# The sigmoid of the output gates as exp(-ln(1 + exp(-z))), with one VectorE operation per tile

## The chip, the cores and the metric

The kernel runs on one core of one Trainium2 chip. A core has a matrix engine (TensorE, here PE, with its weight loads as PEld), a vector engine (VectorE, DVE), an engine for activation functions (ScalarE, ACT), a general engine (GpSimd, POOL), a sync engine that issues transfers (SP) and 16 DMA engines. Each engine works through a queue of its own in order and waits on semaphores for the others. The metric is the device time of one execution in microseconds; the median of the runs counts. The profile is that of one further execution.

## The reference

One decoder layer of width 1024 on one sequence of 2048 positions: a modulated RMSNorm, one input projection, two groups of heads (A: gated linear attention, B: sliding-window attention), one output projection, a gated residual and a last RMSNorm. Both groups' outputs pass a SiLU gate of their own, and that gate is what the change touches.

```
proj = einsum('bsd,de->bse', h, w_in)
gq, gk, gv, ga, gz, sq, sk, sv, sz = split_cols(proj, COL_SIZES)
z = einsum('bsr,rk->bsk', ga, w_decay) + b_decay
log_a = log_sigmoid(z) / GLA_GATE_TAU
o_gla = rmsnorm(gla_chunked(gq, gk, gv, log_a), g_gla_head)
o_gla = o_gla * silu(gz)
o_swa = sliding_window_sink_attention(rope(sq), rope(sk), sv, sinks)
o_swa = o_swa * silu(sz)
x = x + gate * einsum('bse,ed->bsd', concat([o_gla, o_swa]), w_out)
return rmsnorm(x, g_final)
```

gz and sz have 512 columns each, and silu(z) = z * sigmoid(z).

## The kernel before

The 2048 positions are worked in four units of 512. In each unit the input projection runs slot by slot (lines 30 to 42 and 55 to 56): qk0 and qk1, gv0 and gv1, gz0 and gz1 for group A, kv, sq0 and sq1, sz0 and sz1 for group B. Every product of fp32 matrices is made of three matmuls on parts: a high part h and a low part l of each operand (hh and hl for the activations, wh_ and wl_ for the weights). An h part is a rounded copy by ACT, the l part is a subtraction on DVE or POOL. In the first unit the weights are split as they arrive, and the parts are written to memory (wc); later units load the parts. During the last unit late_rows (line 561) loads the output gate's weights and w_out: wor is a piece of w_out as loaded, DVE multiplies it by the gate and subtracts for the low part (woy or wol). Then last_rows and out_tile do the output projection (py) and the last norm, 16 tiles of 128 positions.

The gate slots gz0, gz1, sz0 and sz1 come out transposed, two tiles of 128x512 per slot in PSUM (pt; po in the first unit), so there are 4 x 2 x 4 = 32 gate tiles in all. sink_gz and sink_sz give each to gate_evac (line 804), which copies it to z (the tile zs, six buffers), and makes sigmoid(z) in e (the tile ge, a single buffer). log_sigmoid (line 797) makes log(sigmoid(z)) = min(z, 0) - ln(1 + exp(-|z|)): one DVE instruction makes min(-z, z), ACT takes Exp and Ln, and a second DVE instruction makes the difference. A third ACT instruction, Exp, gives the sigmoid. The product with z is made on POOL for group B, and on DVE together with the head's weight for group A. The same log_sigmoid serves the decay (dz, de, line 935), where the logarithm itself is wanted.

Other names that the rows show: pq are transposed queries, qs their parts, psc the scores, s the scores in SBUF with the maximum mx, its negative nm and the sum den; ppt the transposed probabilities, ph and pl their parts, pp a masked copy of them, ppo their product with the values vs, o the output; kst the keys, pkr their transposes. In group A pk and kn are transposed keys, pc scores, sT their copy, pu the state's update, R and Q the state.

The order of the instructions is planned when the kernel is built. Every operation goes to an object (Order, line 88) with a price; for DVE 0.155 us and one 960th of a us per element of a partition, or one 1920th for a plain copy or an operation with one tensor operand, both in SBUF (lines 366 and 367). A list scheduler with these prices fixes each engine's queue, PE's as well, so that a new price or one instruction fewer can change the order anywhere behind it.

Of the kernel before, what the change touches and what calls it, by code (L numbers as in the profile page):

```python
# [11 lines left out]
AF = mybir.ActivationFunctionType  # L12
ALU = mybir.AluOpType
# [370 lines left out]
def layer_kernel(ctx, tc, x, xT, w_ada, w_gate, b_cols, b_gate, g_cols, c_cols, pos, inv_freq,  # L384
# [3 lines left out]
    V, A, G, SY = [Engine(od, e) for e in ("V", "A", "G", "SP")]  # L388
# [408 lines left out]
    def log_sigmoid(z, e):  # L797

        V.scalar_tensor_tensor(e, z, -1.0, z, op0=ALU.mult, op1=ALU.min)
        A.activation(e, e, AF.Exp)  # L800
        A.activation(e, e, AF.Ln, bias=1.0)
        V.scalar_tensor_tensor(e, z, 0.0, e, op0=ALU.min, op1=ALU.subtract)

    def gate_evac(ps, z, g=None):
        A.copy(z, ps)
        od.lift = 0
        e = near.tile([P, NB], F32, name="ge", tag="ge", bufs=1)
        log_sigmoid(z, e)
        A.activation(e, e, AF.Exp)
        if g is None:  # L810
            G.tensor_tensor(z, z, e, ALU.mult)
        else:
            V.scalar_tensor_tensor(z, z, g, e, op0=ALU.mult, op1=ALU.mult)
# [75 lines left out]
    def sink_gz(pair):  # L889
        def sink(ct, ps):  # L890
            z = near.tile([P, NB], F32, name="zs", tag="zs", bufs=ZS)
            h = 2 * pair + ct
            gate_evac(ps, z, gh[:, h:h + 1])
            gzs[pair, ct] = z
        return sink
# [152 lines left out]
    def sink_sz(kv):  # L1048
        def sink(ct, ps):
            z = near.tile([P, NB], F32, name="zs", tag="zs", bufs=ZS)  # L1050
            gate_evac(ps, z)
            szs[kv, ct] = z
        return sink
# [340 lines left out]
```

## Time and profile before

| | us |
|---|---|
| median of 3 runs | 862.0 (861.47 to 865.98) |
| the profiled execution, whole | 860.93 |
| its span, first to last instruction | 859.2 |
| PE busy in the span | 837.2 |
| DVE busy | 547.5 |
| ACT busy | 493.9 |
| POOL busy | 373.9 |

The span is what the rows speak of; the median lies 1.1 us above the time of the profiled execution. A busy time is the union of an engine's instructions. PE's matmuls overlap in the pipeline, so that the duration of a single one says more than its share of the time; what PE waits for is read from the idle time before a matmul and from the instruction that ended it.

### The profile page before, as it was taken

The numbers are of one execution on the slowest core, as the hardware profiler recorded it, in microseconds if no ns is written. First come the engines' busy times: TensorE is split into PE (matmuls) and PEld (weight loads), VectorE is DVE, ScalarE is ACT, GpSimd is POOL, SyncE is SP. The second block draws the span as 40 slices with busy tenths as digits, with TensorE's granted clock in tenths as the row PEclk, the third lists the DMA queues.
The fourth block names the chain that finished last, engine by engine and source line by source line (L and its number), as shares of the span: only waits on it lengthen the run. The fifth ranks groups of instructions, "written<-read, shape, count | busy, mean of one in ns | idle before, by whom it ended". The sixth has DMA issues, their size and how long they took to land. (4 is left out here: it accounts for less than half of the span.)

```text
span 859.2 us, 14608 instructions
## 1 busy us (share of the span) xinstructions
PE 837.2 (97%) x5150; PEld 733.6 (85%) x5150; DVE 547.5 (64%) x1014; ACT 493.9 (57%) x1214; POOL 373.9 (44%) x450
## 2 busy tenths in 40 slices
PE   8999999999999999999999999999999999999996
PEld 7798879889899888899898989888888788888886
DVE  6995689785555467655438786668767664444442
ACT  4668588894673679645538756455467443333332
POOL 4624256657254265734425664153325442222221
PEclk9999999999999999999999999999999999999998
DMA  8889898774443566554346646569493764444411
GB/s 335 342 309 328 347 340 287 249 250 142 166 164 119 184 209 246 196 174 158 127 172 204 258 163 209 206 216 347 167 317 125 263 208 148 147 147 144 143 70 50
DMA packets 75999, 179.91 MB, mean 209 GB/s; under 512 B 8419, under 2 KB 24854, under 8 KB 72726
## 3 DMA queue, kind: packets, MB, share of 16 engines
q1 hardware_dynamic: 74918, 178.93, 59.2%
q8 instruction: 41, 0.67, 0.3%
q14 instruction: 32, 0.26, 0.1%
q10 hardware_dynamic: 1008, 0.05, 0.1%
HBM read 134.78 MB, written 44.17 MB: 208 GB/s over the span
## 5 line engine op out<-in xcount | busy, mean ns | idle before, releaser
L425 PE MATMUL py<-woh,m 128*128 128x512 f32 (+2 forms) x528 | 161.5, 385 | 0.4 <-ACT zs L378 0.4
L425 PEld LDWEIGHTS py<-woh,m 128*128 128x128 f32 x528 | 98.5, 188 | 20.5 <-ACT zs L378 0.8
L425 PE MATMUL py<-wol,m 128*128 128x512 f32 (+2 forms) x264 | 101.9, 386 | 0.0
L378 POOL TENSOR_TENSOR r<-r,gf 128x512 f32<-128x512 f32 x31 | 45.4, 1466 | 118.3 <-ACT xr L378 118.3
L378 ACT ACTIVATE ge<-ge 128x512 f32<-128x512 f32 x96 | 60.5, 630 | 29.9 <-DVE ge L378 29.2
L425 PE MATMUL pn<-wh_sq,hh 128*128 128x256 f32 x256 | 73.1, 287 | 1.4 <-DVE vs L378 1.4
L425 PE MATMUL pn<-wh_gv,hl 128*128 128x272 f32 (+1 forms) x256 | 73.6, 288 | 0.0
L425 PE MATMUL pn<-wh_gv,hh 128*128 128x272 f32 (+1 forms) x256 | 73.6, 287 | 0.0
L425 PE MATMUL pn<-wl_gv,hh 128*128 128x272 f32 (+1 forms) x256 | 73.4, 287 | 0.0
L425 PE MATMUL pn<-wl_sq,hh 128*128 128x256 f32 x256 | 72.9, 286 | 0.4 <-DVE wl_sq L378 0.3
L425 PE MATMUL pn<-wh_sq,hl 128*128 128x256 f32 x256 | 72.6, 284 | 0.0
L378 DVE TENSOR_TENSOR r<-py,xr 128x512 f32<-128x512 f32 (+2 forms) x33 | 22.3, 675 | 65.1 <-PE py L425 65.1
L378 ACT ACTIVATE s<-s,nm 128x129 f32<-128x129 f32 x128 | 51.2, 401 | 17.7 <-DVE nm L378 17.0
L378 POOL TENSOR_TENSOR o<-o,zs 128x128 f32<-128x128 f32 x64 | 34.5, 560 | 54.5 <-DVE o L378 54.5
L425 PEld LDWEIGHTS py<-wol,m 128*128 128x128 f32 x264 | 49.6, 188 | 9.8 <-issue 0.2
L378 POOL TENSOR_TENSOR qr<-qr,rope 128x256 f32<-128x256 f32 x32 | 26.1, 832 | 64.9 <-DVE rope L378 64.9
L378 POOL TENSOR_TENSOR s<-s,den 128x512 f32<-128x512 f32 x32 | 36.3, 1136 | 38.9 <-DVE den L378 38.8
L425 PEld LDWEIGHTS pn<-wh_sq,hh 128*128 128x128 f32 x256 | 48.7, 191 | 2.8 <-issue 1.8
L425 PEld LDWEIGHTS pn<-wl_sq,hh 128*128 128x128 f32 x256 | 48.8, 191 | 1.9 <-DVE wl_sq L378 0.8
L378 POOL TENSOR_TENSOR xt<-xt,rstd 128x512 f32<-128x512 f32 x27 | 36.2, 1346 | 31.6 <-DMA xt<-in_xT 22.8
L425 PEld LDWEIGHTS pn<-wh_sq,hl 128*128 128x128 f32 x256 | 48.9, 191 | 0.4
L425 PEld LDWEIGHTS pn<-wh_gv,hh 128*128 128x128 f32 x256 | 48.6, 190 | 0.7
(258 smaller groups left out, 2522.7 us busy)
## 6 DMA issues: line engine op xcount, KB each, us to landing
xr<-in_x SPq DMA_DIRECT2D x32, 256.0 KB, 2.8
mr<-mixd SPq DMA_DIRECT2D x16, 512.0 KB, 4.0
out<-r SPq DMA_DIRECT2D x32, 256.0 KB, 2.3
wa<-in_w_ada SPq DMA_DIRECT2D x7, 1024.0 KB, 8.4
xn<-in_x SPq DMA_DIRECT2D x24, 256.0 KB, 4.2
xt<-in_xT SPq DMA_DIRECT2D x24, 256.0 KB, 4.2
wl_sz<-wc SPq DMA_DIRECT2D x12, 512.0 KB, 5.4
wh_sz<-wc SPq DMA_DIRECT2D x12, 512.0 KB, 4.7
```

The costliest lines, as they stand in the source:

```text
L378: return order.add(eng, lambda: real(*args, **kw), dur, ins, outs, lock=lock, nbytes=nbytes)
L425: return od.add("PE", lambda: T.matmul(o, l, r, start=start, stop=stop), dur, [l, r] + ([] if start else [o]), [bank if start and bank is ...
```

## The change

In gate_evac the call of log_sigmoid and the Exp behind it are replaced. One DVE instruction with one tensor operand makes max(z, -87) in e; ACT makes exp(-e), then ln(1 + that), then exp of the negative of that. The kernel's decay keeps log_sigmoid.

```
@@ -805,8 +805,11 @@
         A.copy(z, ps)
         od.lift = 0
         e = near.tile([P, NB], F32, name="ge", tag="ge", bufs=1)
-        log_sigmoid(z, e)
-        A.activation(e, e, AF.Exp)
+
+        V.tensor_scalar(e, z, -87.0, None, op0=ALU.max)
+        A.activation(e, e, AF.Exp, scale=-1.0)
+        A.activation(e, e, AF.Ln, bias=1.0)
+        A.activation(e, e, AF.Exp, scale=-1.0)
         if g is None:
             G.tensor_tensor(z, z, e, ALU.mult)
         else:
```

The planned order changes on every engine. Three places follow; a number behind a name is a buffer's.

The first is in the first unit, where the first low part of probabilities, pl, is made. DVE's queue ahead of it, before:

```order
L378 TENSOR_TENSOR wl_gz_486<-wr_gz_488,wh_gz_485 128x512
L378 TENSOR_TENSOR hl_4_392<-xt_4_393,hh_4_391 128x512
L378 TENSOR_TENSOR wl_gz_486<-wr_gz_489,wh_gz_485 128x512
L378 TENSOR_SCALAR nm<-mx 128x4
L378 SCALAR_TENSOR_TENSOR ge<-zs,ge 128x512
L378 TENSOR_TENSOR pl<-ppt,ph 128x512
```

And now:

```order
L378 TENSOR_TENSOR wl_gz_486<-wr_gz_489,wh_gz_485 128x512
L378 TENSOR_SCALAR nm<-mx 128x4
L378 TENSOR_TENSOR qs<-pq,qs 64x2x128
L378 TENSOR_TENSOR wl_gz_486<-wr_gz_490,wh_gz_485 128x512
L378 TENSOR_TENSOR hl_6_398<-xt_6_399,hh_6_397 128x512
L378 TENSOR_TENSOR pl<-ppt,ph 128x512
```

The gate's instruction is gone from there; a part of the queries and two parts that stood behind pl now stand ahead of it. PE's queue ahead of the matmul that reads this pl (pn is the projection, slot gv1), before:

```order
L425 MATMUL ppo<-ph,vs 128x512
L425 MATMUL pn_491<-wh_gv_415,hl_6_178 128x256
L425 MATMUL pn_491<-wh_gv_415,hh_7_181 128x256
L425 MATMUL pn_491<-wl_gv_416,hh_7_181 128x256
L425 MATMUL pn_491<-wh_gv_415,hl_7_182 128x256
L425 MATMUL pn_493<-wh_gv_415,hh_0_153 128x256
L425 MATMUL pn_493<-wl_gv_416,hh_0_153 128x256
L425 MATMUL ppo<-pl,vs 128x512
```

And now:

```order
L425 MATMUL pn_493<-wl_gv_416,hh_6_177 128x256
L425 MATMUL ppo<-ph,vs 128x512
L425 MATMUL pn_493<-wh_gv_415,hl_6_178 128x256
L425 MATMUL pn_493<-wh_gv_415,hh_7_181 128x256
L425 MATMUL pn_493<-wl_gv_416,hh_7_181 128x256
L425 MATMUL pn_493<-wh_gv_415,hl_7_182 128x256
L425 MATMUL ppo<-pl,vs 128x512
```

It was row 772 of PE's queue, at the beginning of the tile pn_493; it is row 817 now, behind that tile.

The second place is some 30 us earlier, on DVE, where the keys' low parts (kst_201 and kst_203) are made; what is removed and added there, in one piece:

```order
 L378 TENSOR_TENSOR v<-po_257,ort 128x512
+L378 TENSOR_TENSOR kst_201<-pkr,kst_200 64x512
 L378 TENSOR_TENSOR wl_sz_294<-wr_sz_298,wh_sz_293 128x512
 L378 TENSOR_TENSOR wl_sq_404<-wr_sq_405,wh_sq_403 128x512
 L378 TENSOR_TENSOR wl_sq_404<-wr_sq_406,wh_sq_403 128x512
-L378 TENSOR_TENSOR kst_201<-pkr,kst_200 64x512
 L378 TENSOR_TENSOR kst_203<-pkr,kst_202 64x512
-L378 SCALAR_TENSOR_TENSOR ge<-zs 128x512
+L378 TENSOR_SCALAR ge<-zs 128x512
+L378 TENSOR_TENSOR qs<-pq,qs 64x2x128
```

One of the two key parts moves ahead of three subtractions for weights, and a part of the queries follows the gate's instruction directly.

The third place is in the last unit, on DVE, where pieces of w_out (wor) are multiplied between the steps of the sliding-window attention, before:

```order
L378 TENSOR_TENSOR qs<-pq,qs 64x2x128 x2
L378 TENSOR_TENSOR wor_1252<-wor_1252,gate_1221 128x512
L378 TENSOR_TENSOR woy_1254<-wor_1252,wox_1253 128x512
L378 COPY_PREDICATED s<-up_ex,psc 128x2x128
L378 TENSOR_TENSOR qs<-pq,qs 64x2x128 x2
L378 COPY_PREDICATED s<-up_ex,psc 128x2x128
L378 TENSOR_REDUCE mx<-s 128x4
```

And now:

```order
L378 TENSOR_TENSOR qs<-pq,qs 64x2x128 x2
L378 COPY_PREDICATED s<-up_ex,psc 128x2x128
L378 TENSOR_TENSOR qs<-pq,qs 64x2x128 x2
L378 COPY_PREDICATED s<-up_ex,psc 128x2x128
L378 TENSOR_TENSOR wor_1252<-wor_1252,gate_1221 128x512
L378 TENSOR_REDUCE mx<-s 128x4
L378 TENSOR_SCALAR nm<-mx 128x4
L378 TENSOR_TENSOR woy_1254<-wor_1252,wox_1253 128x512
```

The product of the loaded piece goes from between the first and the second pair of qs to behind both.

## Rows read from the trace of the kernel before

**Rows 1.** The page's busy times: us, share of the span, instructions.

```profile
PE 837.2 (97%) x5150; PEld 733.6 (85%) x5150; DVE 547.5 (64%) x1014; ACT 493.9 (57%) x1214; POOL 373.9 (44%) x450
```

**Rows 2.** Busy time by stage: stretch, its length, engines' busy us, PE clock, DMA.

```profile
0.00:51.00 51.00, 47.02 (x237) 39.48 (x238) 42.26 (x71) 29.52 (x62) 25.10 (x35) 1.00 0.83 322
51.00:158.00 107.00, 101.23 (x729) 92.87 (x728) 82.37 (x145) 79.40 (x174) 46.52 (x51) 1.00 0.92 329
158.00:545.00 387.00, 386.61 (x2583) 345.47 (x2582) 243.86 (x471) 248.08 (x638) 198.18 (x260) 1.00 0.53 185
545.00:692.00 147.00, 141.63 (x882) 121.69 (x881) 104.19 (x191) 83.36 (x218) 58.02 (x74) 1.00 0.68 233
692.00:852.00 160.00, 160.00 (x723) 133.59 (x721) 73.10 (x135) 51.96 (x120) 46.10 (x32) 1.00 0.40 136
```

**Rows 3.** Waits of PE: matmul, who ended them, us in total, times, longest.

```profile
PE psc L425 <- DVE qs L378: 2.5, 4, 1.5
...
PE ppo L425 <- POOL pp L378: 1.6, 1, 1.6
PE ppo L425 <- DVE pl L378: 1.6, 1, 1.6
...
PE pn L425 <- DVE vs L378: 1.4, 1, 1.4
PE pq L430 <- DVE kst L378: 1.1, 1, 1.1
PE pk L430 <- DVE qk L378: 0.9, 1, 0.9
```

**Rows 4.** The gate tile's instructions: count, ns min/median/max, first and last start.

```profile
L378 ACT ACTIVATE ge<-ge x96: 613/632/647, 52.9 to 676.5; 128x512 f32<-128x512 f32 x96
L378 DVE SCALAR_TENSOR_TENSOR ge<-zs x32: 673/693/1784, 51.3 to 671.7; 128x512 f32<-128x512 f32 x32
L378 DVE SCALAR_TENSOR_TENSOR ge<-zs,ge x32: 673/691/1702, 55.2 to 673.8; 128x512 f32<-128x512 f32 x32
L378 DVE SCALAR_TENSOR_TENSOR zs<-zs,gh,ge x16: 728/752/1372, 57.8 to 677.2; 128x512 f32<-128x512 f32 x16
```

**Rows 5.** DVE with one operand: one in the timeline, then a group by line.

```profile
49.40 0.43 DVE L378 TENSOR_SCALAR rn<-rr 128x512 f32<-128x512 f32 x1
...
L378 DVE TENSOR_SCALAR r<-r,frr 128x512 f32<-128x512 f32 x15 | 8.2, 548 | 1.6
```

**Rows 6.** Busy time of the gate tile's instructions alone (DVE, ACT, POOL), by stage.

```profile
158.00:545.00 387.00, 44.63 (x50) 37.78 (x60) 13.62 (x10) 1.00 0.53 185
```

**Rows 7.** Timeline near 146: start, us, engine, instruction, [idle before and its end].

```profile
145.62 0.68 DVE L378 SCALAR_TENSOR_TENSOR ge<-zs,ge 128x512 f32<-128x512 f32 x1
146.22 0.68 DVE L378 TENSOR_TENSOR pl<-ppt,ph 128x512 fp32r<-128x512 f32 x1
...
146.95 0.50 PE L425 MATMUL ppo<-pl,vs 128*128 128x512 f32 x1 [1.57 <-DVE pl L378]
```

**Rows 8.** Timeline near 115, the keys' parts.

```profile
112.23 3.49 DVE L378 TENSOR_TENSOR wl_sq<-wr_sq,wh_sq 128x512 fp32r<-128x512 f32 x2
...
115.64 1.40 DVE L378 TENSOR_TENSOR kst<-pkr,kst 64x512 fp32r<-64x512 f32 x2
...
117.19 0.41 PE L430 MATMUL pq<-ident,qr 128*128 128x128 f32 x2 [1.09 <-DVE kst L378]
```

**Rows 9.** Timeline near 636, pieces of w_out between attention steps.

```profile
634.18 0.69 DVE L378 TENSOR_TENSOR wor<-wor,gate 128x512 f32<-128x512 f32 x1 [2.55 <-DMA wor<-in_w_out]
...
636.76 0.87 DVE L378 TENSOR_TENSOR qs<-pq,qs 64x256 fp32r<-64x256 f32 x2
...
637.23 0.51 PE L425 MATMUL psc<-kst,qs 128*128 128x256 f32 x2 [1.51 <-DVE qs L378]
```

**Rows 10.** Timeline near 92, the values' parts.

```profile
91.12 0.35 ACT L378 CAST vs<-pn 128x256 fp32r<-128x256 f32 x1
...
92.05 0.19 PEld L425 LDWEIGHTS pn<-wh_sq,hh 128*128 128x128 f32 x1 [1.60 <-issue]
92.08 0.36 PE L425 MATMUL pn<-wh_sq,hh 128*128 128x256 f32 x1 [1.44 <-DVE vs L378]
```

## The prediction

> **What bounds the kernel now.** First the page's busy times: TensorE (PE) is busy 837.2 of 859.2 us, 97% [rows 1]. Whoever looks for a gain has therefore 22 us of PE idle time to look at, and nothing else, as long as the matmuls stay what they are; the change leaves all of them. Next the busy time by stage [rows 2], where the reader is to subtract PE's busy time from each stretch. From 0 to 51 us, before the first gate tile, 4.0 us are idle (51.00 - 47.02). From 51 to 158, the rest of the first unit, 5.8. From 158 to 545, 0.4 in 387 us. From 545 to 692, the last unit with the loading of w_out beside it, 5.4. From 692 to 852, the output projection, nothing. The last 8 us are the closing normalisation. The change can reach the second, third and fourth stretch only: 11.6 us at most, a floor of about 850 for the median.
>
> Then the list of PE's waits [rows 3], which says who ends them. VectorE (DVE) ends most of what stands there: psc on qs 2.5, ppo on pl 1.6, pn on vs 1.4, pq on kst 1.1, pk on qk 0.9; one, ppo on pp 1.6, is ended by GpSimd. So DVE does matter, but at some ten places, not through its 64% share.
>
> **The edit itself.** Per gate tile, 32 of them, two DVE instructions with two operands go, of 693 and 691 ns at the median [rows 4]. One with one operand comes. The trace has that form at the same size, 128x512 in SBUF: 0.43 us in one row, and 548 ns on the mean of 15 that use a column as scalar [rows 5]. The new one's scalar is a constant, as in the first of the two, so I take 0.43. By medians DVE gets back 0.693 + 0.691 - 0.43 = 0.95 us per tile, 32 x 0.95 = 30.5 us in all. From above: at the longest seen, 1784 ns [rows 4], each new one would cost more than the two together, and DVE would get nothing; I don't take it, since the median is near the shortest (673).
>
> ScalarE (ACT) keeps three activations per tile at 632 ns [rows 4]: a scale of -1 for none, Exp and Ln as before, and the order of the instructions has the same three table loads. What falls away there is the trip to DVE and back between the second and the third. GpSimd (POOL) keeps its 16 products. A -87 clamp is a constant. All this I cost at nothing; it is covered by PE's work, and shown by the third stretch: 50 of the 80 DVE instructions on these tiles lie there, 44.63 us of them [rows 6], while PE idles 0.4 us. So most of what the edit saves is saved where nobody waits: at most 0.4 us of it counts.
>
> **What it moves.** The order of all instructions is planned with prices, and two cheaper instructions shift every engine's queue; the totals of work stay. So the sum goes by PE's waits, place by place.
>
> At 146.95 PE waits 1.57 us for pl [rows 7]. DVE runs ge there from 145.62 and pl right behind it, at 146.22: the removed instruction stood 0.60 us ahead of pl. Now wl_gz, hl and a qs stand ahead of it, but the matmul that reads pl has gone from row 772 of PE's queue to row 817. A PE row takes 386.61 / 2583 = 0.15 us on the mean of the third stretch [rows 2], so it comes some 6 us later: more than pl's delay by qs (half of 0.87, [rows 9]), a wl_gz and an hl (an estimate from the 3.49 us of two such subtractions, [rows 8]: 1.75 each) together, 3.9. I count -1.5.
>
> At 117.19 PE waits 1.09 us for kst, which stands behind two subtractions of 3.49 us [rows 8]. The first kst now goes ahead of those; the second doesn't, and the buffer that PE waits for is free after both. But the waiting transposes stand three matmuls later. Between nothing and all of it, 1.09, and with a wait for qs some 5 us behind it (0.5 of the 2.5 in [rows 3]) whose qs now stands right behind the gate tile's instruction: I count -1.2.
>
> At 637.23 PE waits 1.51 us for qs [rows 9]. Ahead of qs, DVE had been held until 634.18 by a load of w_out (2.55 us idle). Now that qs stands ahead of the load's product; the row maximum mx stays behind it. This wait goes, and mx takes its place as the late one; the transposes that need it come earlier in PE's queue than before. I count half, -0.75; between -1.5 and +2.5, the row's own hold.
>
> At 92.08 PE waits 1.44 us for vs [rows 10], a DVE subtraction that is late because ACT's cast is (91.12). In the new order vs stands even later, behind three more subtractions, but the matmul that waited for it has moved some 40 rows back. Instead the eight pairs of pu, which need kn, come at once; ACT makes kn where it made vs, at about 91.1, so PE waits until about 91.7 (one ACT copy of 0.6). I count -0.3.
>
> pk on qk, 0.9, and ppo on pp, 1.6 [rows 3], I leave: ahead of qk the product zs (752 ns) now stands in place of ge (691) [rows 4], and the order around pp hasn't changed on DVE or PE.
>
> Removed: 1.5 + 1.2 + 0.75 + 0.3 = 3.75 us. Against it stand the waits that a new order makes. The nearest rows are the list itself: waits of 1.1 to 1.6 us at the places where PE's queue runs close behind DVE. I take one of 1.3 us. Net -2.5 us. The sum is made against the profiled execution, span 859.2 and 860.9 in all; the median of the runs is 862.0, 1.1 above it. **859.5 us** for the median.
>
> **A rule that would give more.** Weight loads are busy 733.6 us, 85% [rows 1]. In the stretch from 692 to 852, where PE never waits, their share is 133.59 / 160 = 83% [rows 2]; so 85% is what a PE without waits shows, and no headroom. The Trainium skill, Perfetto Trace Analysis, section Identifying the Most-Contended Engine, calls the share of busy matmuls a bad measure and wants that of weight loads in its place; by that rule 126 us would be open, and a cheaper DVE could give far more than the floor above. The trace doesn't bear it out here, and I give it 0.01.
>
> **Rivals.** (1) *Nothing that lasts*, 0.22: each wait removed is made again nearby, since DVE is late there because loads and ACT are (the 2.55 us hold in [rows 9], the late cast in [rows 10]). For it speaks that only 0.60 us of the 5.4 and 5.8 us idle is seen to stand on the removed instruction itself [rows 7]. 862, between 861 and 863.5.
>
> (2) *DVE was late by its load alone*, 0.15: in the first unit DVE gets back up to eight tiles' 0.95 us, 7.6 in all, and its waits there and in the last unit go: 2.5 + 1.6 + 1.4 + 1.1 + 0.9 and pp's 1.6 behind pl [rows 3], 9.1 us. 853, or 856 when a third is kept. Against it speak the same two rows.
>
> (3) *Slower: PE's queue drawn too near to a DVE that a load holds*, 0.10. In the last unit the planner puts the transposes of s earlier in PE's queue, trusting DVE to have made them. But DVE's queue is in order, and a product that waits for its load of w_out holds all behind it, 2.55 us at one place [rows 9], with mx and what follows behind it now. At two loads of this kind, with the second unit's gains eaten: -2.5 is lost, and 2 x 2.55 = 5.1 comes on top: 867. It decides from the point where PE has less than a hold's length of other matmuls in front of those transposes.
>
> (4) *The change doesn't do what it says*, 0.03: the new instruction takes about as long as the two, at the 1784 ns of [rows 4]. Then DVE is loaded as before while the plan thinks it free: 862 to 864. The Trainium skill, SBUF - State Buffer, section on the two separate sides, says that a DVE instruction in a two-port mode and a GpSimd instruction keep each other out of a shared pair of ports for the whole instruction, as does one with two SBUF inputs. By that rule the new instruction can still be held by the whole of a GpSimd product; the long ends of [rows 4] fit it, the medians say that it is the exception.
>
> **How the numbers follow.** The forecast has the rest, 0.49, with a range of its own from 857.5 to 861.5. What this kernel's measurement can tell from no change is about 0.5%, 4.3 us. Faster by more: rival 2 (0.15), the weight-load rule (0.01) and a little of the forecast, 0.18. Slower by more, above 866.3: most of rival 3, 0.09. The same: 0.73. For 8 in 10 the range reaches from 855, which leaves a good half of rival 2 outside, to 866, which leaves most of rival 3.
>
> **What would show it.** DVE's instructions on the gate tile: 32 of about 0.43 us in place of 64, its busy time down by some 30 us; ACT, POOL and PE's busy time within a few us. PE idle in 158 to 545 still below 1 us. No wait for pl near 146 and none for qs near 637. A wait for kn near 92 in place of that for vs. In the last unit the reader should look for waits on s or qs behind a product of w_out: if they are above 2 us, rival 3 holds. I am wrong on the main point if PE's idle time from 51 to 692 changes by more than 5 us either way, or if the time moves while it doesn't.

## The result and the profile after

The changed kernel takes **854.5 us** at the median of 6 runs (853.26 to 855.31), beside 861.7 us for the kernel before in the same set (859.34 to 865.98): a ratio of 0.9913, 95% interval 0.9894 to 0.9932. It is faster by 7.3 us; the forecast was 859.5 and its range ended at 855.0. The profiled execution took 855.22 us, its span 853.5 us. Four executions among the experiments below, 6 to 92% longer than the others of their kernels at a lower granted clock (0.75 to 0.97, where the others have 0.99 to 1.00), are left out of the medians and ratios.

The page's busy times, which answer to [rows 1]:

```profile
PE 833.1 (98%) x5150; PEld 732.1 (86%) x5150; DVE 510.2 (60%) x982; ACT 493.6 (58%) x1214; POOL 367.4 (43%) x450
```

DVE has 37.3 us less, in 32 instructions fewer; ACT is where it was. The busy time by stage, for [rows 2] (stretch, its length, engines' busy us, PE clock, DMA):

```profile
0.00:51.00 51.00, 44.78 (x230) 37.14 (x231) 42.13 (x68) 28.22 (x60) 24.59 (x35) 1.00 0.81 309
51.00:158.00 107.00, 102.87 (x738) 94.56 (x738) 77.74 (x140) 81.18 (x173) 48.11 (x53) 1.00 0.94 340
158.00:545.00 387.00, 386.74 (x2596) 346.87 (x2594) 222.38 (x459) 247.35 (x642) 193.66 (x260) 1.00 0.54 187
545.00:692.00 147.00, 143.72 (x892) 124.15 (x891) 97.92 (x185) 86.21 (x223) 59.46 (x75) 1.00 0.71 241
```

Subtract PE's busy time again: 6.2, 4.1, 0.3 and 3.3 us are idle, where it was 4.0, 5.8, 0.4 and 5.4. Two things are to be seen. The first stretch, which the change doesn't touch, is slower in this execution than in that of before; the profile of before is the quickest there of all that were taken (the others are 0.2 to 2.1 us later at its end), so that is chance, and the profiles are compared from 51 us on. And behind 51 us the idle time falls by 1.6 + 0.1 + 2.1 = 3.9 us, while the time falls by 7.2: the start of the 237th matmul is 1.5 us later than before, the end is 5.7 us earlier. PE does the same 5150 matmuls in both. So 3.3 us came out of what the trace shows as busy. By stage, from the starts of the matmuls with equal numbers (the 965th, the 3545th, the 4425th): 2.0 us gained up to 158, 2.0 from there to 545, 3.2 up to 692, nothing behind. (A second profiled execution of the changed kernel gives 1.9, 1.6 and 3.9, so a stretch of one trace is known to some 0.7 us.)

PE's waits, for [rows 3] (from 51 to 692 us):

```profile
PE pz L425 <- POOL zs L378: 1.9, 1, 1.9
PE pk L430 <- DVE qk L378: 1.6, 2, 1.3
PE ppo L425 <- POOL pp L378: 1.5, 1, 1.5
PE psc L425 <- ACT s L378: 1.5, 1, 1.5
PE psc L425 <- DVE qs L378: 0.4, 1, 0.4
PE psc L425 <- DVE s L378: 0.3, 1, 0.3
PE pt L425 <- DVE wl_qk L378: 0.2, 1, 0.2
```

Gone are pl (1.6), vs (1.4), kst (1.1) and 2.1 of the 2.5 on qs. pp stands as it did, and pk has grown from 0.9 to 1.6. pz at 77.7 and psc at 138.5 are new. The gate tile's instructions, for [rows 4]:

```profile
L378 ACT ACTIVATE ge<-ge x96: 613/632/667, 53.1 to 667.4; 128x512 f32<-128x512 f32 x96
L378 DVE TENSOR_SCALAR ge<-zs x32: 410/428/1566, 52.7 to 664.7; 128x512 f32<-128x512 f32 x32
```

The median of the new instruction, 428 ns, is the 0.43 us that the prediction took.

### The profile page after: what moved, and what is told of

The parts are those of the page before. It is cut to its first block, busy times and chain, and to the rows that moved or that the text cites. A ratio compares the mean times of both kernels' runs of the same rounds, so it can differ in the third digit from the quotient of the medians.

```text
span 853.5 us, 14606 instructions
## 1 busy us (share of the span) xinstructions
PE 833.1 (98%) x5150; PEld 732.1 (86%) x5150; DVE 510.2 (60%) x982; ACT 493.6 (58%) x1214; POOL 367.4 (43%) x450
## 5 line engine op out<-in xcount | busy, mean ns | idle before, releaser
L378 ACT ACTIVATE ge<-ge 128x512 f32<-128x512 f32 x96 | 60.6, 632 | 16.5 <-DVE ge L378 15.5
L378 POOL TENSOR_TENSOR s<-s,den 128x512 f32<-128x512 f32 x32 | 34.2, 1072 | 48.7 <-DVE den L378 40.7
```

The costliest lines, as they stand in the source:

```text
L378: return order.add(eng, lambda: real(*args, **kw), dur, ins, outs, lock=lock, nbytes=nbytes)
```

## The experiments

Each is compared with the kernel before, run in the same set (862.5, 863.1, 861.9 and 861.9 us in the four sets). Five questions were asked.

**Are they the instructions or the order?** The change does both. To part them, the planner was told the old prices and the old operations, so that the queues of all engines are those of before, and only the instructions differ:

```
-        log_sigmoid(z, e)
-        A.activation(e, e, AF.Exp)
+        two = 0.155 + NB / 960     # the old price
+        V.tensor_scalar(e, z, -87.0, None, op0=ALU.max).dur = two
+        A.activation(e, e, AF.Exp, scale=-1.0)
+        A.activation(e, e, AF.Ln, bias=1.0)
+        od.add("V", lambda: None, two, [z, e], [e], lock=True)   # planned, not issued
+        A.activation(e, e, AF.Exp, scale=-1.0)
```

> The new instructions in the old order: every engine's queue is word for word that of the kernel before, only that the first DVE instruction of each gate tile has one operand and the second is not issued. Theory A (DVE's relief itself): the 30 us that DVE gets back count by themselves, most of the 7.3 us is here, 855 to 857. Theory B (the order): what was gained comes from the new queues; here only the waits directly behind a removed instruction shrink, near 146 from 1.57 to about 1 us and near 598 from 0.94 to about 0.3, so 860 to 861.

Measured: 857.3 us, ratio 0.9942 (0.9922 to 0.9962). The new instructions give 5.2 of the 7.3 us without a single row being moved. Its trace, 3.7 us shorter than that of before, gains 1.9 us up to 158, 0.8 from there to 545 and 1.2 up to 692, by the starts of the matmuls. The counterpart has the changed kernel's queues with the old instructions in them (the second one issued where the third activation stands):

```
-        V.tensor_scalar(e, z, -87.0, None, op0=ALU.max)
-        A.activation(e, e, AF.Exp, scale=-1.0)
+        V.scalar_tensor_tensor(e, z, -1.0, z, op0=ALU.mult, op1=ALU.min).dur = one
+        A.activation(e, e, AF.Exp)
         A.activation(e, e, AF.Ln, bias=1.0)
-        A.activation(e, e, AF.Exp, scale=-1.0)
+        third = A.activation(e, e, AF.Exp)   # issues the second DVE instruction ahead of itself
         ...                                  # not shown: how it does so; one is the new price
```

> The old instructions in the new order: queues as in the changed kernel, but each gate tile has its two DVE instructions of two operands again, the second one put where its third activation stands. Theory A: nothing of the gain is left, 861 to 864, slower where the plan draws PE close to a DVE that now has more to do. Theory B: most of the gain stays, 855 to 857.

Measured: 876.5 us, ratio 1.016 (1.013 to 1.019), far above the times of either theory (A allowed for slower, without a figure). PE's longest waits in its stretch from 158 to 545 us, where before has 0.4 us in all:

```profile
PE psc L427 <- DVE qs L380: 4.2, 6, 1.1
PE ppo L427 <- DVE o L380: 1.3, 1, 1.3
PE po L427 <- DVE o L380: 1.1, 1, 1.1
```

Waits for DVE appear in the stretch that I had taken for covered; by the starts of its matmuls the kernel loses 9.0 us there. The new order is no good by itself: it leans on the instructions being short. (It is one way to put the old instructions in; another place for the second could cost less.)

**Is it DVE's load, or the trip to DVE and back?** Three kernels in the order of before. The first leaves out the second instruction and keeps two operands in the first; the second makes the first cheap and keeps the second; the third keeps two instructions of the old form and size, but the second depends on nothing that ACT makes, nor does ACT wait for it.

```
e5  V.scalar_tensor_tensor(e, z, -87.0, z, op0=ALU.max, op1=ALU.max)
    ... od.add("V", lambda: None, ...)                     # second planned, not issued
e6  V.tensor_scalar(e, z, -87.0, None, op0=ALU.max).dur = two
    ... V.scalar_tensor_tensor(e, z, 0.0, e, op0=ALU.mult, op1=ALU.subtract)
e7  V.scalar_tensor_tensor(e, z, -87.0, z, op0=ALU.max, op1=ALU.max)
    ... nc.vector.scalar_tensor_tensor(z, z, 1.0, z, op0=ALU.mult, op1=ALU.min)
```

> All queues are word for word those of the kernel before, but the second of the two DVE instructions on each gate tile isn't issued; the first keeps its two operands (it makes max(z, -87) in the two-operand form). Theory A (DVE's load): the gain goes with the DVE time that is given back, 32 x 0.69 = 22 of the 30.5 us that gave 5.2 us with both edits in this order, so 0.72 x 5.2 = 3.8 us: 858.7 beside 862.5 for before. Theory B (the trip): what cost was that the second instruction stands on DVE's queue waiting for ACT's logarithm and holds all behind it (the trace of before has 15.0 us of DVE idle time in 12 waits of that kind): all of the 5.2 us comes, 857.3.

> All queues are those of the kernel before; the first DVE instruction on each gate tile has one operand (max(z, -87)) in place of two, the second stays with its two operands and its wait for ACT (it makes 0 * z - ln). Theory A: 32 x 0.26 = 8.4 us of DVE time come back, 0.28 x 5.2 = 1.4 us: 861. Theory B: nothing, 862 to 862.8, since DVE then waits longer for ACT.

> All queues are those of the kernel before and DVE does as many instructions of the same form and size on each gate tile (two with two operands, 128x512), but the second reads and writes z alone and depends on nothing that ACT makes, and ACT's third activation needs nothing of it. DVE's busy time stays at about 547 us. Theory A (load): no gain, 862 to 863. Theory B (the trip): most of the 5.2 us, 857.3 to 858.5.

Measured: 857.4 (ratio 0.9934, 0.9909 to 0.9959); 859.3 (0.9963, 0.9944 to 0.9981); 863.0 (1.0, 0.9982 to 1.0019). The third decides. First the wait of DVE's second instruction for ACT's logarithm in the trace of before (us, times, longest); then the third kernel's busy times, and the one wait for ACT's activations that DVE's instructions on the gate tiles still have there, that of the product zs:

```profile
DVE ge L378 <- ACT ge L378: 15.0, 12, 3.3
...
PE 838.7 (97%) x5150; PEld 735.1 (85%) x5150; DVE 549.0 (64%) x1014; ACT 492.8 (57%) x1214; POOL 374.4 (43%) x450
DVE zs L380 <- ACT ge L380: 3.9, 5, 2.6
```

The 15.0 us of waiting are gone, DVE's load is as before, and so is the time. Theory B falls: without the trip, and with the load kept, nothing was gained, within 1.6 us to either side. Theory A holds in kind. The busy times with the first instruction cheap, with the second left out, and with both (the first experiment):

```profile
PE 835.8 (97%) x5150; PEld 732.3 (85%) x5150; DVE 539.2 (63%) x1014; ACT 494.5 (58%) x1214; POOL 370.8 (43%) x450
...
PE 834.6 (98%) x5150; PEld 733.2 (86%) x5150; DVE 520.6 (61%) x982; ACT 493.5 (58%) x1214; POOL 369.2 (43%) x450
...
PE 836.3 (98%) x5150; PEld 733.6 (86%) x5150; DVE 512.5 (60%) x982; ACT 493.0 (58%) x1214; POOL 365.9 (43%) x450
```

A's proportion doesn't show: 8.3, 26.9 and 35.0 us less of DVE's busy time gave 3.8, 5.6 and 5.2 us by the medians, with intervals of 1.6 to 2.2 us to either side, and the first of them is more than twice what A expected. One rival isn't tested. GpSimd's busy time falls with DVE's, from 373.9 to 370.8, 369.2 and 365.9, though it does the same 450 instructions, and it stays at 374.4 in the kernel that gained nothing. A part of the relief may have reached PE through GpSimd, and no run parts the two.

**Does the covered stretch count?** New instructions in the order of before, on the 20 gate tiles between 158 and 545 us alone, and on the 12 others alone:

```
+        if 6 <= tile < 26:        # the other kernel: if not 6 <= tile < 26
             ...                   # the instructions of the first experiment
+        else:
+            log_sigmoid(z, e)
+            A.activation(e, e, AF.Exp)
```

> The queues of the kernel before, with the new instructions on the 20 gate tiles that lie between 158 and 545 us alone (one operand in the first, the second not issued); the other 12 keep theirs. By the prediction's step (at most 0.4 us of what is saved there counts, since PE idles 0.4 us there): 862.5 to 863, and PE's matmuls of that stretch take as long as before within 0.4 us. By its rival (short delays of PE hide in what the trace shows as busy, since matmul records overlap): the stretch gets 1 to 2 us shorter, 861 to 862.

> The queues of the kernel before, with the new instructions on the other 12 gate tiles alone (6 before 158 us, 6 after 545). By the prediction's step nearly all of the 5.2 us that the new instructions gave in this order: 857.5 to 858.5. By the rival 1 to 2 us less: 859 to 860.

Measured: 860.6 (0.9989, 0.9970 to 1.0008) and 858.5 (0.9971, 0.9958 to 0.9985). The times don't decide: the first lies below both of its expectations and isn't told from no change, and the second lies at the upper end of what the prediction's step gave. But the first one's trace can be laid matmul by matmul on that of before, since PE's queue is the same: from the 965th to the 3545th it takes 1.3 us less. (With the outer tiles alone that stretch takes 0.2 us more.) The gain stands at few places: 15 matmuls start 0.05 us or more closer behind the one ahead, 1.9 us together, 1.4 of it at psc, which reads qs; two, a pms that reads osq and the one behind it, take 0.6 back. The other kernels in this order bear it out: the stretch is 0.8 and 1.3 us shorter in the two without the second instruction on all tiles, 0.2 shorter with the first cheap, and 1.7 longer in the one that keeps the load, 1.0 of it at a single ppo. The first one's busy time there:

```profile
158.00:545.00 387.00, 386.64 (x2588) 346.70 (x2587) 222.35 (x455) 248.92 (x641) 194.71 (x261) 1.00 0.53 187
```

PE idles 0.36 us, where it was 0.39 (387.00 - 386.61, [rows 2]). The stretch got shorter by 1.3 us while its idle time moved by 0.03. One place shows how that can be. Before, at 305.6 (ACT, DVE and PE; start, us, instruction, idle before and its end):

```profile
304.24 0.64 ACT L378 ACTIVATE ge<-ge 128x512 f32<-128x512 f32 x1 [1.69 <-DVE ge L378]
304.77 0.35 ACT L378 CAST qs<-pq 64x256 fp32r<-64x256 f32 x1
...
305.05 0.39 PE L425 MATMUL pt<-hh,wh_qk 128*128 128x512 f32 x1
305.16 0.42 DVE L378 TENSOR_TENSOR qs<-pq,qs 64x256 fp32r<-64x256 f32 x1 [0.52 <-ACT qs L378]
305.63 0.51 PE L425 MATMUL psc<-kst,qs 128*128 128x256 f32 x2 [0.19 <-DVE qs L378]
```

And with the new instructions on the middle tiles:

```profile
303.11 0.65 ACT L380 ACTIVATE ge<-ge 128x512 f32<-128x512 f32 x1
303.64 0.35 ACT L380 CAST qs<-pq 64x256 fp32r<-64x256 f32 x1
...
305.59 0.40 PE L427 MATMUL pt<-hh,wh_qk 128*128 128x512 f32 x1
305.83 0.40 PE L427 MATMUL psc<-kst,qs 128*128 128x256 f32 x2
```

From one matmul's start to the next it was 305.63 - 305.05 = 0.58 us and is 305.83 - 305.59 = 0.24; 0.34 us were lost, and 0.19 of them show as idle, because the record of the matmul ahead lasts 0.39 us where the next could start after 0.24. A delay below 0.15 us shows as nothing there. The chain behind it: ACT's activation had waited 1.69 us for DVE's first instruction on the gate tile, the cast of qs stands behind it in ACT's queue, and DVE's own qs and PE come after that. In the whole trace ACT waited 29.2 us for ge in 28 places before, and 15.5 in 14 in the changed kernel.

**Was the order a lucky one?** The changed kernel's instructions, with another price told to the planner for the new one (it took 0.422 us), and the changed kernel again:

```
-        V.tensor_scalar(e, z, -87.0, None, op0=ALU.max)
+        V.tensor_scalar(e, z, -87.0, None, op0=ALU.max).dur = 0.45    # 0.548, 0.40
```

> The changed kernel's instructions without a difference, but the planner is told 0.450 us for the new DVE instruction where it took 0.422; every engine's order changes somewhat (PE's in some 380 of 5150 rows). If the changed kernel's time comes from the cheaper instructions, any order that is planned with them gives about the same, a ratio of 0.989 to 0.993 to before. If its order was a lucky one (7.3 us beside the 5.2 that the instructions gave in the old order), this one falls short: 0.994 to 0.998.

> The changed kernel itself, beside the two others of this set. If its order is an ordinary one: 0.991, and the two others within 0.002 of it. If it is a lucky one: 0.991, and the two others at 0.994 to 0.998.

> The changed kernel's instructions without a difference; the planner is told 0.548 us for the new DVE instruction (the mean of 15 with a column as scalar in the trace of before), in place of 0.422. Ordinary order: 0.989 to 0.993. Lucky order: 0.994 to 0.998.

> The changed kernel's instructions without a difference; the planner is told 0.400 us for the new DVE instruction. Ordinary order: 0.989 to 0.993. Lucky order: 0.994 to 0.998.

Measured: 857.4 (0.9951, 0.9928 to 0.9975); the changed kernel 855.6 (0.9931, 0.9903 to 0.9958); 854.0 (0.9905, 0.9881 to 0.9929); 853.4 (0.9906, 0.9878 to 0.9934). The price of 0.45, taken alone, fell where a lucky order would have put it; but the two others are below the changed kernel, by 0.0025 where 0.002 was allowed. Three orders of four lie at 0.990 to 0.993, one at 0.995: the changed kernel's order isn't a lucky one, as far as four orders can tell. The 2 us between it and the first experiment (0.9942) are at the edge of what the intervals part, and whether the plan with right prices earns them stays open. Where the gain lies is a matter of the order too. By the starts of the matmuls, in one trace each, against before:

| us gained | to 158 | to 545 | to 692 |
|---|---|---|---|
| the changed kernel | 2.0 | 2.0 | 3.2 |
| priced 0.45 | 3.5 | -0.7 | 3.6 |
| priced 0.548 | 4.1 | -0.2 | 3.9 |
| priced 0.40 | 4.6 | 1.3 | 3.9 |

The last unit gains in every order; the middle stretch, in two of four, gains nothing.

**Does DVE still count, and is there a better kernel?** One operand or two in the one instruction that is left, no DVE instruction at all (ACT reads z; the bound at -87 is left out) in an order planned for it, the same in the order of the changed kernel, and a version in which DVE makes the bound while it takes the tile out of PSUM, so that ACT's copy goes:

```
e3  V.scalar_tensor_tensor(e, z, -87.0, z, op0=ALU.max, op1=ALU.max)
e4  A.activation(e, z, AF.Exp, scale=-1.0)             # no DVE instruction
e8  od.add("V", lambda: None, 0.155 + NB / 1920, ...)  # planned, not issued; ACT reads z
e9 -A.copy(z, ps)
   +V.tensor_scalar(z, ps, -87.0, None, op0=ALU.max)
   +A.activation(e, z, AF.Exp, scale=-1.0)
```

> As changed, but the one DVE instruction has two operands (max(z, -87) taken with z twice), 0.69 in place of 0.43 us; the order is planned anew for that price. Theory A: 0.69 of the 0.95 us per tile is kept, so about 5.3 of 7.3 us, 856 to 857. Theory B: a new order, any time from 853 to 863, not tied to DVE's busy time.

> As changed without the clamp: no DVE instruction at all, ACT takes Exp of -z straight from the copied tile; planned anew. It leaves out the guard for z below -87. Theory A: another 0.43 us per tile, 14 us in all, comes off DVE, and the time falls on, to 851 to 853. Theory B: any time from 851 to 862.

> All queues are word for word those of the changed kernel, but the one DVE instruction on the gate tiles isn't issued: ACT's first activation reads z itself (the bound at -87 is left out, which this input doesn't reach). Another 32 x 0.43 = 13.7 us of DVE time are given back and one more step falls away ahead of ACT. Theory A (load): 0.45 of what the first 30.5 us gave in a fixed order, 2.3 us: a ratio of 0.989 to before, 852 to 853. Theory C (what DVE ended of PE's waits is used up): the same as the changed kernel, ratio 0.991 to 0.993.

> An attempt at a better version: the DVE instruction reads the tile from PSUM and makes z = max(z, -87) there, in place of ACT's copy of the tile; ACT's first activation reads z. DVE has the same count of instructions as the changed kernel, ACT has 32 copies fewer. If ACT's load counts as DVE's did: 850 to 853. If not, 854 to 856, since ACT ends few of PE's waits once it is under way. If DVE is now late with emptying PSUM, since an ACT copy of 128x512 takes its place on a busier queue: above 858.

Measured: 860.6 (0.9974, 0.9957 to 0.9992); 857.5 (0.9928, 0.9901 to 0.9954); 853.1 (0.9876, 0.9852 to 0.9900); 851.5 (0.9886, 0.9865 to 0.9907). Between the second and the third nothing differs but the order, and they are 0.5% apart; the first is slower in its own order than the same instructions in that of before (e5, 0.9934). So an order alone can take away about half of what the edit gives, and the first two miss what theory A expected. In the changed kernel's order another 16.2 us off DVE's busy time (510.2 to 494.0) still gain, 0.9876 beside 0.9913 and 0.9931, as theory A had it. But this kernel also spares ACT its wait for DVE's instruction (15.5 us in the changed kernel), so that it doesn't show by itself that it is DVE's load that still counts.

The last one keeps the bound and is the best of those that do, but not by a margin that the runs show: 3 us below the changed kernel's 854.5, in another set, with intervals that overlap (0.9865 to 0.9907 beside 0.9894 to 0.9932), and the changed kernel's own instructions reach 0.9905 in other orders. What of it is ACT's lighter load and what the order, no run parts. Its first unit, and ACT's load on the page:

```profile
51.00:158.00 107.00, 107.00 (x764) 98.44 (x764) 84.14 (x146) 79.73 (x175) 49.56 (x56) 1.00 0.95 346
...
PE 834.3 (98%) x5150; PEld 732.5 (86%) x5150; DVE 515.4 (61%) x982; ACT 475.8 (56%) x1182; POOL 361.8 (43%) x450
```

PE idles not at all from 51 to 158, where 5.8 us were idle before; 7.0 us are gained up to there, 0.8 lost in the middle stretch and 3.9 gained in the last unit.

## Why the prediction was wrong

**The edit's own cost: right in kind.** 32 instructions of 428 ns in place of 64. Their gain was 37.3 us of DVE's busy time, not 30.5, in the main because the sum went by medians: the means were 867 and 837 ns before (27.7 and 26.8 us in all) and are 612 ns now (19.6 us). That makes 34.9; the other 2.4 came off DVE's other instructions.

**The waits taken one by one: right in part, and in part by luck.** The wait for pl (1.57), that for kst (1.09) and that for qs at 637 (1.51) are gone. The pl one was put down to the order; it fell to 0.7 us in the old order too. pk on qk (now 1.3 at the longest) and ppo on pp (1.5) stayed, as said. At 92 the wait for vs went, and the wait for kn that was to stand in its place didn't come: ACT made kn at 92.59, and PE had other matmuls until it needed kn at 93.23. In the first unit I had 3.0 us, or 1.7 if the new wait of 1.3 falls there, and it was 2.0. That is luck: the wait for vs gave over 1 us more than I counted, and the new waits, 1.9 and 1.5, took 2.1 more.

**The step that failed** is "most of what the edit saves is saved where nobody waits: at most 0.4 us of it counts", with the floor "22 us of PE idle time to look at, and nothing else" above it. Idle time of PE is not a bound on its delays, since the records of its matmuls overlap (0.39 us long, 0.23 to 0.24 apart). The stretch from 158 to 545 gave 2.0 us in the changed kernel where the sum had nothing, 1.3 when it alone got the new instructions, and lost 9.0 when the old instructions stood in the new order; in two of the three other orders of the new ones it gave nothing. In all 7.2 us came behind 51 us where the sum had 2.45, and 3.3 of the 4.75 that it lacked show as no idle time: 1.9 in this stretch, 1.1 in the last unit, 0.3 in the first. The overlap was known when the sum was made, and the sum went by idle time all the same. The sign named for it, that the time moves while idle time doesn't, came half: idle time fell by 3.9 us. It is the reason for the floor that falls, not its number: no kernel here has a median below 850.

**The second miss is a size, and the larger one**, the last unit: 0.75 was counted, 3.2 came, and other orders gave 3.6 to 3.9. I gave half for 637 and it was the whole; and the small waits that stand between 545 and 692 in the trace of before were not in the sum at all:

```profile
PE py L425 <- ACT zs L378: 0.4, 1, 0.4
PE ppt L430 <- POOL s L378: 0.3, 1, 0.3
PE psc L425 <- DVE s L378: 0.2, 1, 0.2
```

None of them is left: pk and ppo are PE's only waits there now, pk 0.7 longer than before. With the 0.3 of a second qs, the small ones are 1.2 us of idle time. In all 2.1 us of idle time went there; the rest of the 3.2 has again no idle time to it.

**The rivals.** *DVE was late by its load alone*, priced at 853 to 856 and given 0.15, is what the runs come nearest to: most of the gain comes without a move in the order (the first experiment) and none without DVE's load going down (the third of the three on the trip); the part of GpSimd in it is open. What I held against it, that few of the idle microseconds stand on the removed instruction itself, was no evidence: an instruction delays what stands behind it on DVE, and through ACT's queue what stands behind ACT's wait, not only its neighbour. But it reached its price by another way than the one I gave, the listed waits of the first and last unit alone. *Slower* didn't come. The old instructions in the new order show that an order drawn close behind a busy DVE can cost more than the 5 us that it said (14 us), but most of that, 9.0, lies between 158 and 545, and not at the loads of the last unit that it named. Of the rule that the prediction took from the Trainium skill, Perfetto Trace Analysis, section Identifying the Most-Contended Engine, the runs bear out the half that calls the share of busy matmuls a bad measure: 3.3 us came out of it. The half that looks at weight loads found no support: they are 732.1 us, 1.5 less than before.

## What to carry to other kernels

When the bounding engine's records overlap, its idle time is a lower bound on what it loses: lay the start times of its instructions on the best pitch that the trace shows, and a stretch that is "99.9% busy" may still hold gains. Here a load taken off a helper engine paid at many small lags behind it, through the other helpers' in-order queues too, so such a load is better priced by the stage than by the waits in a list alone. And where a planner sets the order, run the edit once in the old order: it tells the edit's worth from the new order's, and orders of the same instructions here lay up to 0.5% apart, with their gains in different stretches.

## What the runs showed of the hardware

A DVE instruction can be held until a GpSimd one ends. The new wait of 1.5 us at 138.5 comes from such a pair; POOL, DVE, then ACT and PE behind them in the changed kernel's timeline, and DVE's negations as a group (count, ns min/median/max, first and last start):

```profile
134.88 2.96 POOL L378 TENSOR_TENSOR xt<-xt,rstd 128x512 f32<-128x512 f32 x2 [0.28 <-DMA xt<-in_xT]
...
136.64 1.23 DVE L378 TENSOR_SCALAR nm<-mx 128x4 f32<-128x4 f32 x1
...
137.96 0.40 ACT L378 ACTIVATE s<-s,nm 128x129 f32<-128x129 f32 x1 [3.83 <-DVE nm L378]
...
138.49 0.71 PE L425 MATMUL psc<-kst,qs 128*128 128x256 f32 x4 [1.48 <-ACT s L378]
...
L378 DVE TENSOR_SCALAR nm<-mx x32: 136/170/1228, 136.6 to 645.3; 128x4 f32<-128x4 f32 x32
```

The negation of 128x4 elements, 170 ns at the median, lasts 1.23 us and ends at 136.64 + 1.23 = 137.87, as the GpSimd products end at 134.88 + 2.96 = 137.84. The Trainium skill, SBUF - State Buffer, section on the two separate sides, says that a DVE instruction in a two-port mode and a GpSimd instruction keep each other out for the whole instruction, and that only the shared pair of ports is contended for; the rows agree. They agree in the version that reads PSUM too, where the same operation takes the tile from there: it is longer at the median than from SBUF (428 ns) but never long:

```profile
L378 DVE TENSOR_SCALAR zs<-pt x28: 660/691/692, 117.2 to 659.9; 128x512 f32<-128x512 f32 x28
```

660 to 692 ns in 28 cases, in 16 of which GpSimd was busy for 0.38 us or more of the time. The SBUF form of the changed kernel goes from 410 to 1566 ns; 12 of the 32 are longer than 500, and a GpSimd instruction overlaps each of these.
